# A triangular inverse's transposed products: every second block written to the other half of the partitions

## The chip, the cores and the metric

The kernel runs on one core of a Trainium2 chip. A core has a matrix engine (TensorE, PE in the profile, with its weight loads as PEld), VectorE (DVE), ScalarE (ACT), GpSimd (POOL) and a queue engine (SP) that issues most transfers. TensorE multiplies 128 partitions by up to 128 columns; it can be used as four quarters of 64 by 64, addressed by the half of the partitions from which the operands come (rows) and the half of the partitions to which the product goes (columns). Products land in PSUM, in banks of 512 f32 per partition. The metric is the time of one execution in microseconds, lower is better; several runs give a median.

## What is computed

One decoder layer on 256 tokens of width 1024. Two branches work on the same normalised input: an RWKV-7 time mixing with 8 heads of 64, and a softmax attention with 8 heads of 64 (with 256 tokens its one block is the causal block itself). They are gated, projected and added, and a gated MLP of width 2816 follows. The change lies in the time mixing, whose core is a recurrence over tokens:

```python
def step(state, inp):
    r_t, w_t, k_t, v_t, a_t, b_t = inp
    sa = jnp.einsum('bhvk,bhk->bhv', state, a_t)
    state = (state * w_t[:, :, None, :] + sa[..., None] * b_t[:, :, None, :]
             + v_t[..., None] * k_t[:, :, None, :])
    return state, jnp.einsum('bhvk,bhk->bhv', state, r_t)
```

The kernel doesn't step through tokens. It cuts the 256 tokens into 4 chunks of 64; in a chunk, the terms `sa` depend on one another through a triangular 64x64 matrix, and solving for them takes the inverse of one such matrix for each of 8 heads and 4 chunks: 32 inverses.

## The kernel before, in words

**The inverse.** The tile `X` holds, for each of the 32 matrices, the inverse as far as it is known, on side 0 plain and on side 1 transposed. Its shape is 128 partitions by 2 sides by 16 slots `u` by 64 columns; a matrix sits in one half of the partitions, `bsl(a)` for `a` of 0 or 1, so two matrices share a slot. Slot `u = 8q + i` belongs to group `q` of two, with `i` from 0 to 7. The diagonal blocks of 16 are inverted first, on VectorE, and brought into place by transfers. Then the blocks are joined to 32 and to 64 by products. `below` (line 764) multiplies the matrices in `G` by side 0 of `X`; `masked` (line 772) keeps the part that belongs to the block below the diagonal, in a tile `P`; `plain` (line 781) makes the product for side 0, and `turned_` (line 789) the one for side 1; `added` (line 777) adds a product from PSUM to `X`. The joining to 64 needs only side 1 at the end, so `plain` is called once and `turned_` four times: line 830 for group 0 and line 836 for group 1 (to 32), line 840 for both (to 64). After that, `X` side 1 is used at line 906 in the loop over the 4 chunks.

`below` and `plain` go through `QA`, the four pairs of row half and column half, so successive products fall into four quarters; each of their two PSUM banks takes the products of one row half. `turned_` reads partitions `bsl(a)` and writes `bsl(a)` of one bank, so it uses two quarters: 16 products (8 slots by 2 halves) of f32 64x64 by 64x64.

**PSUM.** Banks come from three tags: `acc` with 3 buffers for the large projections, `ch` with 3 (function `chp`, called through `bank` in this stage), and `at` with 2 (function `atp`), which the attention uses: its `scores` (line 992) take both `at` buffers for each of three parts, which VectorE (line 1002) and, in two parts, ScalarE (line 1005) empty; its transposes (line 1027) and weighted sums (line 1039) take them later.

**The order of the work.** The Python program runs generators as threads: `chain` (the time mixing), `gn` (its group norms), `att` (the attention) and `bulk` (large projections that fill the time). Each `yield cost, lat` tells the planner how much TensorE time the step took and after how long its results are there; the planner (lines 1118 to 1133) always runs the first thread in the list whose due time has passed, so bulk work fills the waiting time. A bulk step here is the eight matmuls of lines 302 and 304 and the four of line 307, with a cost of 0.33 times 4. The framework then sets each engine's order: by default the program's, but an instruction that is not ready by the framework's own timing (an operand, or a free buffer of its tag) is overtaken by later ones that are. Each engine runs its order strictly. VectorE also splits weights for the bulk work (line 269), ScalarE rounds them (line 259), and both serve the attention's softmax (lines 1010 to 1017).

**Behind the stage.** In the loop over chunks, line 910 and line 909 copy the solved terms, lines 916 and 928 make the new state and the output, lines 856 to 866 normalise it (line 864 on GpSimd), and line 873 transposes it on TensorE.

Of the kernel before, what the change touches and what calls it, by code (L numbers as in the profile page):

```python
# [13 lines left out]
OP = mybir.AluOpType  # L14
# [23 lines left out]
def body(tc, x, positions, norm1_g, w_in, rwkv_mu, w_decay_up, decay_bias, w_aaa_up,  # L38
# [3 lines left out]
    act, dve, pool, pe = nc.scalar, nc.vector, nc.gpsimd, nc.tensor  # L42
    ctx = ExitStack()
    with ctx:
# [9 lines left out]
        def b8(name, shape):  # L54
            return sb.tile(shape, F32, name=name, tag="b8", bufs=5)
# [14 lines left out]
        def acc(name="acc"):  # L70
            return ps.tile([128, 512], F32, name=name, tag="acc", bufs=3)

        def chp(name="ch"):
            return ps.tile([128, 512], F32, name=name, tag="ch", bufs=3)
# [410 lines left out]
        with tc.manual_schedule(engines={E.PE, E.Activation, E.DVE, E.Pool}):  # L485
            p = first_steps()
# [24 lines left out]
        p = acc()  # L511
# [12 lines left out]
        def bsl(q):  # L524

            return slice(64 * (1 - q), 64 * (1 - q) + 64)
# [28 lines left out]
        def chain():  # L555
# [35 lines left out]
            p = chp("pss")  # L591
            for t in range(2):
                for ct in range(4):
                    i = 8 * t + 2 * ct
                    pe.matmul(p[:, i:i + 2], sq[:, ct, t * 128:t * 128 + 128], bones[:, 0:128:64],
                              start=True, stop=True)
# [9 lines left out]
            for j in range(2):  # L606
                p = chp("prx").rearrange("p (a t c) -> p a t c", a=2, t=2)
# [59 lines left out]
            for g in range(2):  # L667
                pg = [[p.rearrange("p (u i) -> p u i", u=4) for p in pj] for pj in banks("pgr")]
                for ct in (2 * g, 2 * g + 1):
                    for c in range(4):  # L670
                        u = 4 * ct + c
                        for q, hs in PAR:
                            pe.matmul(pg[ct % 2][q][:, c], kb(q, u), AR[hs, u].rearrange("p a i -> p (a i)"),
                                      start=True, stop=True)
# [39 lines left out]
            X = b8("X", [128, 2, 16, 64])  # L714
# [21 lines left out]
            for c in range(4):  # L736
                for ct in range(4):
                    for q, hs in PAR:
                        pe.matmul(pv[c // 2][hs, c % 2, ct], ch4(zv)[hs, ct, c], ident[hs, hs],
                                  start=True, stop=True)  # L740
# [20 lines left out]
            def bank(nm):  # L761
                return chp(nm).rearrange("p (u n) -> p u n", u=8)

            def below():
                p = [bank("pp") for _ in range(2)]
                for i in range(8):
                    for q, a in QA:
                        u = 8 * a + i
                        pe.matmul(p[q][bsl(a), i], G[q][bsl(q), u, 0:64], X[bsl(q), 0, u], start=True, stop=True)
                return p  # L770

            def masked(p, mk):
                P = b2("P", [128, 8, 64])
                dve.tensor_tensor(P, p, mk[:, None, :].to_broadcast([128, 8, 64]), op=OP.mult)
                return P

            def added(side, g, p):
                v = X[:, side, 8 * g:8 * g + 8]
                dve.tensor_tensor(v, v, p, op=OP.add)

            def plain(P):

                p = [bank("px") for _ in range(2)]
                for i in range(8):
                    for q, a in QA:
                        pe.matmul(p[a][bsl(q), i], X[bsl(a), 1, 8 * q + i], P[q][bsl(a), i], start=True, stop=True)
                return p

            def turned_(q, P):

                p = bank("px")
                for i in range(8):
                    for a in range(2):
                        pe.matmul(p[bsl(a), i], P[bsl(a), i], X[bsl(a), 1, 8 * q + i], start=True, stop=True)
                return p

            yield 0, 11.0
            yield 0, 2.0
# [5 lines left out]
            for j in range(2):  # L804
                p, pg = chp(), chp("pg")
# [21 lines left out]
            P = [masked(pp[q], m16) for q in range(2)]  # L827
            yield 1.4, 2.0
            px = plain(P)
            pt = turned_(0, P[0])  # L830
            for a in range(2):
                added(0, a, px[a])
            added(1, 0, pt)
            yield 2.4, 2.5
            pp = below()
            pt = turned_(1, P[1])
            P = [masked(pp[q], m32) for q in range(2)]
            added(1, 1, pt)
            yield 2.4, 2.5
            pt = [turned_(q, P[q]) for q in range(2)]  # L840
            for q in range(2):
                added(1, q, pt[q])
            yield 2.3, 2.5

            ny = {}
            yah_, yal = by("yah", dt=F32R), by("yal", dt=F32R)
# [38 lines left out]
            for c in range(4):  # L885
# [4 lines left out]
                if St is not None:  # L890
                    for j in range(2):
                        for q, a in QA:
                            ct = 2 * j + a
                            pe.matmul(pz[q][bsl(a), j], AR[half(q), 4 * ct + c, 0], St[half(q), ct],
                                      start=j == 0, stop=False, skip_group_check=True)
                    for j in range(2):
                        for q, a in QA:
                            ct = 2 * j + a
                            pe.matmul(py[q][half(a), j], AR[half(q), 4 * ct + c, 1], St[half(q), ct],
                                      start=False, stop=False, skip_group_check=True)  # L900
# [3 lines left out]
                for j in range(2):  # L904
                    for q, a in QA:
                        pe.matmul(pu[a][bsl(q), j], X[bsl(a), 1, 8 * q + 4 * j + c], Z0[bsl(a), q, c, j],
                                  start=St is None and j == 0, stop=False, skip_group_check=True)
# [4 lines left out]
                if c < 3:  # L912
                    pS = chp("pS").rearrange("p (a n) -> p a n", a=8)
                    for h in range(8):
                        ct, q = divmod(h, 2)
                        pe.matmul(pS[half(q), ct], KBt[c][:, ct, half(q)], VU[:, c, q, ct],
                                  start=True, stop=True)
# [7 lines left out]
                for j in range(2):  # L925
                    for q, a in QA:
                        ct = 2 * j + a
                        pe.matmul(py[q][half(a), j], G[q][:, gslot(ct, c), 64:128], VU[:, c, q, ct],
                                  start=False, stop=j == 1, skip_group_check=True)
# [187 lines left out]

        now_t = 0.0
        threads = [["chain", chain(), 0.0], ["bulk", bulk(), 0.0]]
        while threads:  # L1120
            th = next((h for h in threads if h[2] <= now_t), None)
# [112 lines left out]
        for j in range(11):  # L1234
# [13 lines left out]
            for m in range(2):  # L1248
                n = 2 * j + m
# [29 lines left out]
        for f, is_ in ((0, (0,)), (1, (0,)), (0, (1,)), (2, (0,)), (1, (1,)), (2, (1,)), (3, (0, 1)), (4, (0, 1))):  # L1279
            t, hf = divmod(min(f, 3), 2)  # L1280
            ts = slice(t * 128, t * 128 + 128)
            c0, n = ((0, 512), (0, 256), (256, 256))[max(f - 2, 0)]
# [37 lines left out]
```

## Time and profile before

| what | value |
| --- | --- |
| median of 3 runs (410.5 to 411.31) | 411.17 us |
| profiled execution, its own time | 410.45 us |
| its span, first to last instruction | 408.5 us |
| TensorE busy | 402.3 us, 98% |
| VectorE, ScalarE busy | 325.3 us (80%), 232.3 us (57%) |
| granted TensorE clock, mean | 1.000 |

A row of the timeline gives the start and the duration in microseconds, the engine, the line, the operation, out<-in, the tile of the array (as `64*64`), partitions x elements and, behind `x`, how many records were merged; in brackets stands the idle time of the engine before it and what ended it. A row of the chain gives start, duration, engine, tile and line. A row of the groups has, behind the bar, the busy time in us and the mean of one in ns.

### The profile page before, as it was taken

To read this page: it belongs to the slowest core of one execution; us is meant where nothing else is said; L and a number is where in the kernel's file an instruction comes from. 1 tells how busy PE (TensorE), PEld (TensorE's weight loads), DVE (VectorE), ACT (ScalarE), POOL (GpSimd) and SP (SyncE) were. 2 spreads that over 40 slices of the span, in tenths; PEclk is the share of its full clock that TensorE was granted. 3 is DMA by queue.
4 is the path that set the end of the run, shared out by engine and by line. 5 is a ranking of instruction groups with operands and counts; after the bars stand their busy time and mean duration, and the time that the engine had idled before them with its cause. 6 is when DMAs were issued, how large, how long until landed. Compare 5 with 4: busy or idle time off the path is not lost.

```text
span 408.5 us, 8160 instructions
## 1 busy us (share of the span) xinstructions
PE 402.3 (98%) x3202; PEld 354.8 (87%) x3202; DVE 325.3 (80%) x565; ACT 232.3 (57%) x387; POOL 39.8 (10%) x65
## 2 busy tenths in 40 slices
PE   8999999999999999999999999999999999999996
PEld 4999989888988989999988888888888888888885
DVE  3988999889679786777974899968769678697694
ACT  6799655474546756444553876645545555465450
POOL 8900070000500010020010100000000000000000
PEclk9999999999999999999999999999999999999999
DMA  8944555563783353466663556666665656656612
GB/s 248 311 160 155 156 164 157 149 170 93 167 230 95 102 154 104 131 206 189 197 194 121 174 188 195 217 208 184 209 179 171 215 186 197 203 164 206 200 53 103
DMA packets 61990, 70.53 MB, mean 173 GB/s; under 512 B 9421, under 2 KB 52243, under 8 KB 61952
## 3 DMA queue, kind: packets, MB, share of 16 engines
q1 hardware_dynamic: 61104, 69.54, 56.7%
q0 software_dynamic: 832, 0.47, 0.6%
q8 instruction: 25, 0.41, 0.4%
q14 instruction: 13, 0.11, 0.1%
q10 hardware_dynamic: 16, 0.00, 0.0%
HBM read 68.56 MB, written 1.44 MB: 171 GB/s over the span
## 4 chain that ended last, share of the span: by engine, by line
PE 94%; DVE 2%; ACT 2%; issue 1%; POOL 0%; ACTq 0%
PE acc L1206 15%; PE acc L302 8%; PE acc L1211 8%; PE acc L304 8%; PE acc L307 7%; PE at L1206 5%; PE acc L323 5%; PE acc L327 4%; PE f L1228 4%; PE acc L324 4%; PE f L1230 4%; PE f L1226 4%; PE at L1211 2%; PE acc L461 1%; PE idle L109 1%
## 5 line engine op out<-in xcount | busy, mean ns | idle before, releaser
L259 ACT CAST whi<-raw 128x1024 fp32r<-128x1024 f32 x120 | 125.7, 1051 | 114.1 <-PE acc L1206 22.2
L269 DVE TENSOR_TENSOR wlo<-raw,whi 128x1024 fp32r<-128x1024 f32 x121 | 148.3, 1229 | 30.0 <-PE acc L1211 12.2
L1206 PE MATMUL acc<-hx,whi 128*128 128x512 f32 x264 | 68.2, 393 | 0.0
L302 PE MATMUL acc<-hx,whi 128*128 128x256 f32 x232 | 59.1, 290 | 0.0
L304 PE MATMUL acc<-hx,whi 128*128 128x256 f32 x232 | 56.6, 279 | 0.0
L1206 PEld LDWEIGHTS acc<-hx,whi 128*128 128x128 f32 x264 | 47.0, 188 | 8.1
L302 PEld LDWEIGHTS acc<-hx,whi 128*128 128x128 f32 x232 | 43.7, 188 | 2.1 <-issue 1.2
L304 PEld LDWEIGHTS acc<-hx,whi 128*128 128x128 f32 x232 | 43.7, 188 | 0.1
L1211 PEld LDWEIGHTS acc<-h,wlo 128*128 128x128 f32 x264 | 37.1, 188 | 3.6
L1211 PE MATMUL acc<-h,wlo 128*128 128x256 f32 x264 | 37.9, 279 | 0.0
L307 PE MATMUL acc<-hx,wlo 128*128 128x256 f32 x232 | 36.0, 278 | 0.0
L1228 PE MATMUL f<-whi,hb 128*128 128x512 f32 x80 | 31.2, 390 | 0.0
L1230 PE MATMUL f<-wlo,hb 128*128 128x512 f32 x80 | 31.2, 390 | 0.0
L1226 PE MATMUL f<-whi,hb 128*128 128x512 f32 x80 | 31.2, 389 | 0.0
L307 PEld LDWEIGHTS acc<-hx,wlo 128*128 128x128 f32 x232 | 31.0, 189 | 0.0
L1206 PE MATMUL at<-hx,whi 128*128 128x512 f32 x88 | 24.0, 392 | 0.0
L1216 DVE TENSOR_REDUCE an<-acc 128x256 f32<-128x512 f32 x22 | 14.2, 685 | 9.3 <-PE acc L1211 9.3
L1206 PEld LDWEIGHTS at<-hx,whi 128*128 128x128 f32 x88 | 16.4, 188 | 3.6
L323 PE MATMUL acc<-whi,hx 128*128 128x512 f32 x48 | 19.1, 398 | 0.0
L324 PE MATMUL acc<-whi,hx 128*128 128x512 f32 x48 | 18.7, 390 | 0.0
L1230 PEld LDWEIGHTS f<-wlo,hb 128*128 128x128 f32 x80 | 15.0, 188 | 3.1
L1226 PEld LDWEIGHTS f<-whi,hb 128*128 128x128 f32 x80 | 15.0, 188 | 2.8
(324 smaller groups left out, 698.6 us busy)
## 6 DMA issues: line engine op xcount, KB each, us to landing
raw<-in_w_ffn_up_dram SPq DMA_DIRECT2D x44, 512.0 KB, 4.0
raw<-in_w_in_dram SPq DMA_DIRECT2D x37, 512.0 KB, 4.4
raw<-in_w_ffn_down_dram SPq DMA_DIRECT2D x22, 512.0 KB, 3.9
raw<-in_w_out_dram SPq DMA_DIRECT2D x8, 512.0 KB, 3.8
x<-in_x_dram SPq DMA_DIRECT2D x8, 256.0 KB, 4.2
early<-in_w_in_dram SPq DMA_DIRECT2D x4, 512.0 KB, 7.6
raw<-in_w_branch_b_dram SPq DMA_DIRECT2D x4, 512.0 KB, 3.6
raw<-in_w_branch_a_dram SPq DMA_DIRECT2D x4, 512.0 KB, 4.8
```

The source lines that it names most:

```text
L259: act.copy(wide(hi, k, c), spread(raw, k, c))
L269: eng.tensor_tensor(wide(lo, k, c), spread(raw, k, c), wide(hi, k, c).bitcast(F32), op=OP.subtract)
L302: pe.matmul(om, wh[:, k, ms], xh[:, k0 + k], start=k0 + k + m == 0, stop=False, skip_group_check=True)
L304: pe.matmul(om, wh[:, k, ms], xl[:, k0 + k], start=False, stop=False, skip_group_check=True)
L307: pe.matmul(om, wl[:, k, ms], xh[:, k0 + k], start=False, stop=k0 + k == nk - 1 and m == n - 1, skip_group_check=True)
L323: pe.matmul(ps_[t], xh[:, K, ts], wh[:, k], start=K == 0, stop=False)
L324: pe.matmul(ps_[t], xl[:, K, ts], wh[:, k], start=False, stop=False)
L1206: pe.matmul(ps_[m], wh[:, k, m * 128:m * 128 + 128], hx[:, k0 + k].rearrange("p a s -> p (a s)"), start=k0 + k == 0, stop=False, skip_grou ...
L1211: pe.matmul(ps_[m][:, 0:S], wl[:, k, m * 128:m * 128 + 128], h2[k0 // 4][:, k], start=False, stop=k0 + k == 7, skip_group_check=True)
L1226: pe.matmul(fin[f], hb[:, 0, i, ts], wh[:, 0, cs], start=st, stop=False, skip_group_check=f == 3)
L1228: pe.matmul(fin[f], hb[:, 1, i, ts], wh[:, 0, cs], start=False, stop=False, skip_group_check=f == 3)
L1230: pe.matmul(fin[f], hb[:, 0, i, ts], wl[:, 0, cs], start=False, stop=False, skip_group_check=f == 3)
```

## The change

`turned_` takes two banks instead of one, one of tag `ch` and one of tag `at`, each holding 4 slots. Slots with even `i` go to the first bank, into the same half of the partitions as before; slots with odd `i` go to the second bank, into the other half. A new function `crossed` takes the place of `added` for side 1: one add of 4 slots over all 128 partitions for the even slots, and for the odd ones two adds of 4 slots, each over 64 partitions, which read PSUM in one half and `X` in the other. The three yields behind the products get other costs and due times.

```diff
             def turned_(q, P):
 
-                p = bank("px")
+                p = [f("px").rearrange("p (u n) -> p u n", u=8) for f in (chp, atp)]
                 for i in range(8):
                     for a in range(2):
-                        pe.matmul(p[bsl(a), i], P[bsl(a), i], X[bsl(a), 1, 8 * q + i], start=True, stop=True)
+                        pe.matmul(p[i % 2][bsl(a ^ i % 2), i // 2], P[bsl(a), i], X[bsl(a), 1, 8 * q + i],
+                                  start=True, stop=True)
                 return p
+
+            def crossed(q, p):
+                v = X[:, 1, 8 * q:8 * q + 8:2]
+                dve.tensor_tensor(v, v, p[0][:, 0:4], op=OP.add)
+                for a in range(2):
+                    v = X[bsl(a), 1, 8 * q + 1:8 * q + 8:2]
+                    dve.tensor_tensor(v, v, p[1][bsl(1 - a), 0:4], op=OP.add)
@@
             pt = turned_(0, P[0])
             for a in range(2):
                 added(0, a, px[a])
-            added(1, 0, pt)
-            yield 2.4, 2.5
+            crossed(0, pt)
+            yield 1.9, 2.8
             pp = below()
             pt = turned_(1, P[1])
             P = [masked(pp[q], m32) for q in range(2)]
-            added(1, 1, pt)
-            yield 2.4, 2.5
+            crossed(1, pt)
+            yield 1.9, 2.8
             pt = [turned_(q, P[q]) for q in range(2)]
             for q in range(2):
-                added(1, q, pt[q])
-            yield 2.3, 2.5
+                crossed(q, pt[q])
+            yield 1.2, 2.8
```

## The prediction

> **What bounds the kernel now.** First the page's busy times, then the matmul engine's rows in order of time, then its waits, then the chain of work that ended last.
>
> ```profile
> PE 402.3 (98%) x3202; PEld 354.8 (87%) x3202; DVE 325.3 (80%) x565; ACT 232.3 (57%) x387; POOL 39.8 (10%) x65
> ...
> q8 instruction: 25, 0.41, 0.4%
> ```
>
> PE is the bound: busy in 402.3 of 408.5 us. Work taken off it counts, unless it then waits. The timeline of PE shows the stage of the change (each f32 matmul appears as two records, so the 16 products of one `turned_` call are 32):
>
> ```profile
> 114.29 1.16 PE L769 MATMUL pp<-X,G 64*64 64x64 f32 x64
> ...
> 117.35 1.16 PE L999 MATMUL ps<-qkT,qkT 64*128 64x128 f32 x16
> 118.44 1.16 PE L786 MATMUL px<-P,X 64*64 64x64 f32 x64
> 119.42 0.75 PE L794 MATMUL px<-X,P 64*64 64x64 f32 x20
> 120.56 0.56 PE L794 MATMUL px<-X,P 64*64 64x64 f32 x12 [0.39 <-issue]
> 121.06 0.39 PE L302 MATMUL acc<-hx,whi 128*128 128x256 f32 x1
> ...
> 124.09 1.16 PE L769 MATMUL pp<-X,G 64*64 64x64 f32 x64
> 125.07 0.98 PE L794 MATMUL px<-X,P 64*64 64x64 f32 x28
> 126.21 0.33 PE L794 MATMUL px<-X,P 64*64 64x64 f32 x4 [0.16 <-issue]
> 126.47 1.13 PE L999 MATMUL ps<-qkT,qkT 64*128 64x256 f32 x8
> ...
> 130.47 2.08 PE L794 MATMUL px<-X,P 64*64 64x64 f32 x64
> 132.48 0.38 PE L302 MATMUL acc<-hx,whi 128*128 128x256 f32 x1
> ...
> 148.40 0.41 PE L873 MATMUL pc<-ident,yc 128*128 128x128 f32 x2 [0.75 <-DVE yc L866]
> ```
>
> Line 786 uses four quarters and gets through 64 records from 118.44 to 119.42: 15 ns each. Line 794 uses two and needs 130.47 to 132.48 for 64: 31 ns each. After its start-up PE stands still three times in the whole run, and all three are in these rows: 0.39 and 0.16 us inside line 794, for no wait that the profile names, and 0.75 us at line 873, the group norm's transposes, for VectorE. How that last wait comes about is in the chain that ended last:
>
> ```profile
> 129.90 1.06 ACT whi L259
> 130.95 0.28 ACT sc L1005
> 131.25 1.23 DVE mx L1010
> ...
> 133.19 1.68 ACT sc L1014 x7
> ...
> 137.46 0.34 DVE sc L1002
> ...
> 146.76 1.05 POOL st L864
> 147.83 0.43 DVE yc L866
> ...
> 148.40 0.41 PE pc L873 x2
> 148.81 0.12 PE acc L302
> ```
>
> From about 129 to 148.4 us the chain runs over ACT and DVE (attention's softmax and, behind it in the queues, the first group norm), not over PE. So **the changed products lie just ahead of a stretch in which PE has 0.75 us to spare**; after 148.4 us PE never waits again. The end moves by as much as the row at 148.40 moves, corrected for bulk work done before it.
>
> **The change, part by part.** *The array.* If all four quarters run at line 786's pace, each of the four calls takes 0.5 us for 1.0: 128 records times (31 - 15) ns = -2.0 us of PE. That price is of the same tile size, type and order of quarters as lines 769 and 786, so I take it whole; the lower bound is no saving.
>
> [...] Lines 769 and 786 give each row half its own bank, while the new code lets both row halves write both banks. [...]
>
> ```profile
> 158.33 0.87 PE ppt L1027 x8
> ```
>
> A full-array f32 record of 128 columns takes 0.87 / 8 = 109 ns here, so one of 64 columns would take 54 if it were alone; line 794's 31 are less, so its two quarters already overlap in one bank.
>
> *The first call's gap.* 6404 matmuls and loads over 25 instruction transfers are 256 each, 128 pairs; from the gap before 120.56 to the one before 126.21 lie 12 + 24 + 64 + 28 = 128 records. So both gaps look like the wait for the next block of code. The first is bound to a time (120.5), not to PE: the 20 records ahead of it gain 0.31 us and the gap grows by 0.31. The second gap of 0.16 goes, by the next point.
>
> *The planner.* After the first product step the chain is due again in 2.8 instead of 2.5. A bulk step costs 0.33 x 4 = 1.32, so two of them (2.64) covered 2.5 and do not cover 2.8: a third runs before `below`. Following the due times on, every later step keeps its order. So one bulk step moves ahead of line 873. It is no added work; its length is the distance from 148.81 above to the row below, 1.38 us.
>
> ```profile
> 150.19 0.11 PE acc L302
> ```
>
> *The second bank.* `turned_` now takes one of the two `at` buffers, which the attention scores (line 999) take both of. This is a wait that was not there. VectorE's rows:
>
> ```profile
> 120.14 1.28 DVE L1002 TENSOR_TENSOR sc<-ps,cmask 128x512 f32<-128x512 f32 x2
> ...
> 122.59 1.87 DVE L779 TENSOR_TENSOR X<-X,px 128x512 f32<-128x512 f32 x3
> 124.38 0.16 DVE L1011 TENSOR_SCALAR mx<-mx 128x8 f32<-128x8 f32 x1
> ...
> 125.59 1.28 DVE L774 TENSOR_TENSOR P<-pp,m 128x512 f32<-128x512 f32 x2
> 126.78 0.68 DVE L779 TENSOR_TENSOR X<-X,px 128x512 f32<-128x512 f32 x1
> 127.80 0.20 DVE L1016 RECIPROCAL sm<-sm 128x8 f32<-128x8 f32 x1 [0.34 <-ACT sc L1014]
> 128.03 1.23 DVE L1017 TENSOR_TENSOR sc<-sc,sm 128x1024 f32<-128x1024 f32 x1
> 129.18 0.75 DVE L1002 TENSOR_TENSOR sc<-ps,cmask 128x256 f32<-128x256 f32 x2
> ...
> 134.88 0.18 DVE L1016 RECIPROCAL sm<-sm 128x4 f32<-128x4 f32 x1 [1.02 <-ACT sc L1014]
> ```
>
> The first call's odd products need the first score bank read: 120.14 + 0.68 = 120.8, while PE is there at 119.5. With 28 records left it ends near 121.2, against 121.06 now: the first call gives nothing (+0.5 back, which covers the 0.31 above too). The second call finds its bank free. But the scores behind it need that bank back: masks (1.28 us from 126.6) and then the adds, to about 129.0, while PE is there at 127.1. That is at most 1.9 us. The pair of calls needs the scores read, and the last scores, one bulk step behind the pair, need six adds done: about 1 us. Behind a PE wait stands the whole in-order engine, bulk matmuls first. These waits total 0 to 4 us: 0 if bulk matmuls are placed ahead of the blocked ones, which the trace shows elsewhere: line 1027's second group, which needs an `at` buffer too, stands inside a bulk step (between lines 304 and 302).
>
> ```profile
> 154.68 0.11 PE acc L304
> 154.79 0.64 PE ppt L1027 x4
> 155.43 0.12 PE acc L302
> ```
>
> Split scores then lose their overlap, under 0.5 us each. I take 1.0 beside the first call.
>
> *VectorE.* Each call's add of 0.62 (1.87 / 3) becomes three adds of 256 elements. No row shows one that reads PSUM in the other half; bounds for a half add are a copy of half the partitions and half that width (273 ns), and the full 512-wide add of line 779 (0.68 us above):
>
> ```profile
> L910 DVE COPY VU<-pb 64x128 f32<-64x128 f32 x4 | 0.9, 273 | 0.0
> L693 DVE TENSOR_TENSOR xgh<-xg,xgh 32x256 fp32r<-32x256 f32 x2 | 0.8, 418 | 0.0
> ```
>
> So 0.27 to 0.68 each; the nearest is 0.42 at 32 partitions (fewer partitions do not shorten it), 0.37 back to back as at line 1002. A call costs 1.1 instead of 0.62: +2.0 us of DVE in all (0.9 to 4.4). The page's share would hide it, but here it stands in the chain: +0.5 ahead of line 1011, whose exponentials now end at 128.3; masks and adds, a bulk step later, hold lines 1016 and 1017 until about 129; so the next scores are read 0.5 to 1.2 us later. The pair's +1.0 falls partly into the 1.02 us for which DVE waits before the next line 1016. I take **0.9 us for line 866 and so for line 873**.
>
> [...]
>
> **The sum**, in the profiled execution (span 408.5, time 410.45, 0.72 below the 411.17 median of the runs). PE, which is there at 148.40 - 0.75 = 147.65 now, reaches line 873 at 147.65 + 1.38 - 2.0 + 0.5 - 0.16 + 1.0 = 148.4. Its data come at 148.40 + 0.9 = 149.3: the later one decides. The end moves by 149.3 - 148.40 - 1.38 = **-0.5 us**: 409.95 by its own time, 410.7 by the median. Most of the saving is spent waiting at line 873.
>
> **Rivals.** *All of it arrives*: the instructions' placing puts line 873 or the blocked scores behind more bulk work, so PE never waits: -2.0 and the gaps, some banks lost: -1.2 to -2.2, say -1.8, 409.4. For it: line 1027's case; against it: the present 0.75 us wait was not placed away. *The shared bank makes it slower*: scores in place wait for the adds, 1.9 us and then 1 to 2 us, while PE stands. The place is the two lines 999 behind the calls; it decides once these waits pass 2.4 us, because then PE reaches line 873 (147.4 and the waits) after 148.40 + 1.38 = 149.78. With 4 us, PE is there at 147.4 + 4 = 151.4 and the end is 151.4 - 149.78 = +1.6; with 3.5, +1.1: 412.3. For it: the buffers are two and DVE's queue there is full; against: placement. *No fourfold overlap*: array saving nought, DVE's cost stays: without waits for banks PE arrives at 147.65 + 1.38 - 0.16 = 148.9, with 1.5 us of them at 150.4; the data come at 149.3, so the end moves by -0.5 to +0.6, say +0.3, 411.5. Against it: line 769.
>
> **How the numbers follow.** A measurement here tells about 0.2% (0.8 us) from no change. Most of it lost at line 873: 0.47, own range 409.9 to 411.3, of which 0.10 is faster than that bound. All of it: 0.26, faster. Shared bank: 0.20, of which 0.18 is slower. No overlap: 0.07, of which 0.02 is slower. Sum: faster 0.36, same 0.44, slower 0.20. The range runs from the second case's middle to the third's: 409.1 to 412.3.
>
> **What would show it.** Line 794's records 15 to 16 ns apart right; 31 would mean no overlap. Three bulk steps between the first call and `below`. Adds near 0.4 us. Line 873 waiting 0.9 us or more says that the saving went there; no wait there means the second case; idle time at line 999 or 794 put to DVE means the third. The forecast is wrong if placement shifts other stages, which I cannot read from this trace.

## The result, and the profile after

The change makes the kernel slower: a median of 416.19 us over 4 runs (415.79 to 417.26), against 410.84 (409.96 to 411.31) for the kernel before, also over 4 runs. The ratio is 1.0134, with a 95% interval of 1.0111 to 1.0156. That is 5.4 us slower where 0.5 us faster was forecast, and above the range's 412.3. The profiled execution took 416.06 us (410.45 before). In the experiments below, one run of e2 took 804.8 us, for a reason that the record doesn't show, and isn't counted.

In the rows below, lines behind the changed functions have moved: line 999 is now 1007, 1002 is 1010, 1010 is 1018, 1016 and 1017 are 1024 and 1025, 866 and 873 are 874 and 881. Line 800 is the add of the even slots, line 803 the two half adds of the odd ones.

First the page of the kernel after: the span, the busy times, and the granted clock in 40 slices (the clock that TensorE was given, in tenths of full speed; 9 is 90% or more).

```profile
span 414.3 us, 8169 instructions
...
PE 404.2 (98%) x3202; PEld 356.2 (86%) x3202; DVE 329.1 (79%) x573; ACT 232.6 (56%) x387; POOL 38.8 (9%) x65
...
PEclk9999999999999899999999999999999999999999
```

The span grew by 5.8 us, but TensorE's busy time grew too, by 1.9, although its instructions are the same 3202 and the changed products became shorter. Something makes other matmuls longer, and the one slice with a clock of 8 says where to look. The matmul engine's rows in order of time, through the stage:

```profile
115.14 1.16 PE L769 MATMUL pp<-X,G 64*64 64x64 f32 x64
...
120.27 0.28 PE L794 MATMUL px<-X,P 64*64 64x64 f32 x4
121.39 0.68 PE L794 MATMUL px<-X,P 64*64 64x64 f32 x28 [0.83 <-DVE sc L1010]
...
126.43 1.16 PE L769 MATMUL pp<-X,G 64*64 64x64 f32 x64
127.41 0.65 PE L794 MATMUL px<-X,P 64*64 64x64 f32 x32
127.99 1.13 PE L1007 MATMUL ps<-qkT,qkT 64*128 64x256 f32 x4
129.05 0.38 PE L302 MATMUL acc<-hx,whi 128*128 128x256 f32 x1
...
133.03 1.32 PE L1007 MATMUL ps<-qkT,qkT 64*128 64x256 f32 x4 [2.79 <-DVE X L803]
134.28 1.22 PE L307 MATMUL acc<-hx,wlo 128*128 128x256 f32 x4
...
137.66 1.16 PE L794 MATMUL px<-X,P 64*64 64x64 f32 x64
138.75 0.38 PE L302 MATMUL acc<-hx,whi 128*128 128x256 f32 x1
...
140.33 0.69 PE L1007 MATMUL ps<-qkT,qkT 64*128 64x256 f32 x2
141.65 1.10 PE L1007 MATMUL ps<-qkT,qkT 64*128 64x256 f32 x6 [0.63 <-DVE mx L1019]
...
155.68 0.41 PE L881 MATMUL pc<-ident,yc 128*128 128x128 f32 x2 [0.54 <-DVE yc L874]
```

The array did nearly what was forecast: the pair of calls takes 137.66 to 138.75, 1.09 us for 64 records, where it took 2.01; the second single call takes 0.58 for 32. But TensorE stops 0.83, 2.79 and 0.63 us, and each time it is held by the second bank: the first call waits until VectorE has read the scores, then twice the scores wait for VectorE. And four bulk matmuls of line 307 need 1.22 us at 134.28, where a whole bulk step of twelve took 1.38 before. The windows (stretch, its length, busy time and count of PE, its loads, VectorE, ScalarE, GpSimd; then the granted clock as a share of full speed, the DMA share and GB/s) show why:

```profile
133.00:134.00 1.00, 0.96 (x4) 0.67 (x4) 0.34 (x1) 0.37 (x1) 0.00 (x0) 0.89 0.00 0
134.00:135.00 1.00, 1.00 (x4) 0.72 (x4) 0.42 (x1) 0.15 (x1) 0.00 (x0) 0.50 0.00 0
...
133.90:137.30 3.40, 3.40 (x16) 3.02 (x15) 1.64 (x2) 0.38 (x2) 0.00 (x0) 0.52 0.00 0
...
138.00:139.00 1.00, 1.00 (x59) 0.93 (x51) 1.00 (x2) 0.34 (x1) 0.00 (x0) 1.00 0.00 0
```

Right behind the stop of 2.79 us the array runs at half its clock for some 3.4 us, which loses about 1.7 us of work. TensorE counts as busy in all of the 3.40 us, at a clock of 0.52, so the page's 98% hides this.

Why the stop is so long stands in VectorE's rows:

```profile
125.58 2.35 DVE L269 TENSOR_TENSOR wlo<-raw,whi 128x1024 fp32r<-128x1024 f32 x2
128.93 0.20 DVE L1024 RECIPROCAL sm<-sm 128x8 f32<-128x8 f32 x1 [1.00 <-ACT sc L1022]
129.17 1.23 DVE L1025 TENSOR_TENSOR sc<-sc,sm 128x1024 f32<-128x1024 f32 x1
130.41 1.29 DVE L774 TENSOR_TENSOR P<-pp,m 128x512 f32<-128x512 f32 x2
131.61 0.41 DVE L800 TENSOR_TENSOR X<-X,px 128x256 f32<-128x256 f32 x1
132.04 0.85 DVE L803 TENSOR_TENSOR X<-X,px 64x256 f32<-64x256 f32 x2
132.92 0.42 DVE L1010 TENSOR_TENSOR sc<-ps,cmask 128x256 f32<-128x256 f32 x1
```

`below` is done at 127.4, but its masks (line 774) start at 130.41. In VectorE's order of instructions the softmax's reciprocal and division now stand **ahead** of the masks; before, the masks came first (125.59) and the division after them (128.03). VectorE waits 1.00 us for ScalarE's exponentials, divides, and only then masks and adds; the scores get their bank at 132.9. TensorE, also in order, has bulk work only until about 130.2.

**The balance**, between line 769 and line 881, which lay 34.11 us apart and now lie 40.54 apart. The bulk step that moved into it accounts for 1.38, which comes back behind line 881; +5.05 stay. Waits: 0.83 + 2.79 + 0.63 + 0.54 = 4.79 for 0.39 + 0.16 + 0.75 = 1.30, +3.49. Half clock: +1.7. Array: -1.9 (without their stops the first call, the second and the pair took 1.25, 1.24 and 2.01, and take 0.90, 0.58 and 1.09). The remaining 1.8 fits the scores: eight records at line 999 in one go took 1.13; cut in two by the bank they take 1.13 + 1.32, and for the last part 0.69 + 1.10, together +2.0, of which 0.2 is the half clock once more. The other 0.8 of the span is the later start, 115.14 for 114.29, before any changed instruction; the wait at line 414, far ahead of the stage, alone runs from none (before) to 1.6 us (e7 below), so I don't count it to the change.

### The profile page after: what moved, and what is told of

Read it like the earlier page. It is cut to its first block, busy times and chain, and to the rows that moved or that the text cites. A ratio compares the mean times of both kernels' runs of the same rounds, so it can differ in the third digit from the quotient of the medians.

```text
span 414.3 us, 8169 instructions
## 1 busy us (share of the span) xinstructions
PE 404.2 (98%) x3202; PEld 356.2 (86%) x3202; DVE 329.1 (79%) x573; ACT 232.6 (56%) x387; POOL 38.8 (9%) x65
## 4 chain that ended last, share of the span: by engine, by line
PE 83%; DVE 7%; DMA 5%; SPq 2%; issue 1%; ACT 0%; POOL 0%; DVEq 0%; ACTq 0%
PE acc L1214 15%; PE acc L302 8%; PE acc L1219 7%; PE acc L307 7%; PE acc L304 7%; PE at L1214 5%; PE f L1236 4%; PE f L1238 4%; PE f L1234 4%; PE acc L323 3%; PE acc L324 3%; PE acc L327 3%; DVE wlo L269 3%; PE at L1219 2%; DMA raw<-in_w_in_dram 2%; SPq L720 2%
## 5 line engine op out<-in xcount | busy, mean ns | idle before, releaser
L302 PE MATMUL acc<-hx,whi 128*128 128x256 f32 x232 | 59.7, 292 | 0.0
L304 PE MATMUL acc<-hx,whi 128*128 128x256 f32 x232 | 57.3, 281 | 0.0
L307 PE MATMUL acc<-hx,wlo 128*128 128x256 f32 x232 | 37.0, 282 | 0.0
```

Source lines behind the costliest of these rows:

```text
L302: pe.matmul(om, wh[:, k, ms], xh[:, k0 + k], start=k0 + k + m == 0, stop=False, skip_group_check=True)
L304: pe.matmul(om, wh[:, k, ms], xl[:, k0 + k], start=False, stop=False, skip_group_check=True)
L307: pe.matmul(om, wl[:, k, ms], xh[:, k0 + k], start=False, stop=k0 + k == nk - 1 and m == n - 1, skip_group_check=True)
```

## The experiments

The theory after this profile: three things have to come together. The faster array brings TensorE early to a bank it shares with the attention; the extra bulk step, which the new due times call for, shifts the division ahead of the masks; the cut adds load VectorE. Rivals: the shared bank alone, the due times alone, the added VectorE work alone, or the clock. All twelve kernels compute the whole layer. "Before" is the median of the kernel before in the same job. The ratio and its interval are estimated from all the counted runs, and can differ by 0.1% from the quotient of the two medians; differences in us in the text are the ratio's, times 411.

| run | median us | before us | ratio (95%) |
| --- | --- | --- | --- |
| e1_acc | 413.81 | 410.96 | 1.0079 (1.006 to 1.0098) |
| e2_yields | 410.86 | 410.96 | 1.0003 (0.9992 to 1.0014) |
| e3_bank | 411.63 | 410.96 | 1.0021 (1.0008 to 1.0033) |
| e4_oldyields | 411.74 | 410.96 | 1.0019 (1.0009 to 1.003) |
| e5_adds_yields | 412.14 | 410.56 | 1.0029 (1.0014 to 1.0044) |
| e6_acc_oldyields | 410.60 | 410.56 | 0.9996 (0.9983 to 1.0009) |
| e7_fill | 414.98 | 410.56 | 1.0116 (1.0089 to 1.0144) |
| e8_pair | 410.68 | 410.56 | 1.0003 (0.9991 to 1.0015) |
| e9_order | 412.05 | 410.52 | 1.0043 (1.0028 to 1.0059) |
| e10_order_acc | 412.74 | 410.52 | 1.0063 (1.0037 to 1.009) |
| e11_pool_before | 411.12 | 410.52 | 1.0013 (0.9996 to 1.003) |
| e12_pool_acc | 410.99 | 410.52 | 1.0015 (1.0003 to 1.0026) |

### The second bank from another tag

The kernel after, with the second bank of `turned_` from the projections' tag:

```diff
-                p = [f("px").rearrange("p (u n) -> p u n", u=8) for f in (chp, atp)]
+                p = [f("px").rearrange("p (u n) -> p u n", u=8) for f in (chp, acc)]
```

> The changed kernel with one word changed: the second bank of the turned products comes from the acc buffers (3, for the large projections) and not from the at buffers that the attention scores use. Theory 1 (the scores behind the second turned product wait on PE for its bank, 2.8 us, and the array's clock falls behind that wait): no idle row at line 1007, granted clock 1.00 all through, 4.5 to 6.5 us of the 5.4 come back, -1.5 to +0.8 us against the kernel before. Theory 2 (VectorE's eight extra adds are what costs): still +3 us or more, as the adds are all there. Theory 3 (the new due times, by one more bulk step ahead of below): still +3 us or more.

It gives back 2.3 us (1.0134 to 1.0079, times 411), and no score waits for a bank any more. But 3.2 us remain, where theory 1 expected 0.8 at most. TensorE stops further on, at the new state of the recurrence, for the late copies of the solved terms (here lines 917 and 918). The matmul engine's rows and the windows:

```profile
142.43 0.33 PE L924 MATMUL pS<-VU,KBt 128*64 128x64 f32 x2 [1.33 <-ACT VU L917]
143.61 1.01 PE L924 MATMUL pS<-VU,KBt 128*64 128x64 f32 x13 [0.86 <-DVE VU L918]
```

```profile
143.00:150.00 7.00, 6.39 (x51) 6.27 (x52) 4.63 (x11) 3.33 (x11) 0.00 (x0) 0.51 0.55 153
150.00:152.00 2.00, 2.00 (x44) 1.81 (x44) 1.37 (x2) 1.83 (x3) 0.00 (x0) 1.00 0.00 0
```

Again the clock halves, now for nearly 7 us, which loses about 3.4 in this execution (415.05 us, the longest of the six; its mean clock is 0.991, as in one other, while the remaining four have 0.996). So the bank shared with the scores isn't the whole cause, and the half clock isn't tied to that place.

### The due times alone

The kernel before, with nothing but the new yields (`yield 1.9, 2.8` twice, `yield 1.2, 2.8`):

> The kernel before with only the three new yields: two quarters, one bank, four plain adds. Theory 1: no shared bank, so within 0.8 us of before; the group norm's wait on PE may move by some tenths. Theory 2: within 0.8 us. Theory 3 (due times alone): +3 us or more.

No difference: 1.0003. The extra bulk step by itself costs nothing, since on TensorE it only changes places. But it already turns VectorE's order round: the division stands ahead of the masks.

```profile
128.02 1.22 DVE L1017 TENSOR_TENSOR sc<-sc,sm 128x1024 f32<-128x1024 f32 x1
129.16 1.28 DVE L774 TENSOR_TENSOR P<-pp,m 128x512 f32<-128x512 f32 x2
```

Here no score stands for it, since none needs a bank from the calls. The same order stands in e1, e5 and e7, which have the new due times too; in e3, e4, e6 and e8, where the step ahead of `below` keeps its old due time, the masks come first, as before.

### The bank alone

The kernel before, in its two quarters and with its due times, but every odd slot in a bank of tag `at`, and each add cut into two:

```diff
-                        pe.matmul(p[bsl(a), i], P[bsl(a), i], X[bsl(a), 1, 8 * q + i], start=True, stop=True)
+                        pe.matmul(p[i % 2][bsl(a), i // 2], P[bsl(a), i], X[bsl(a), 1, 8 * q + i],
+                                  start=True, stop=True)
```

> The kernel before with only the second bank: odd slots go to an at buffer, in the same half of the partitions, so two quarters as before, and two adds of four slots each in place of one of eight; old yields. Theory 1: PE waits at the scores for the bank, but less than 2.8 us, since without the extra bulk step VectorE's order has the masks ahead of the softmax division: +0.5 to +2.5 us. Theory 2: four more adds of about 0.1 us each beyond what they replace: within 0.8 us. Theory 3: within 0.8 us.

Slower by 0.9 us (1.0021). There is no stop at the scores; they are split (four records from 126.95, four from 128.56), and there is no wait at the group norm's transposes; the transposes come 34.97 us after line 769 where they came 34.11 after it. So the bank has a price, but a sixth of what the change costs.

### All of the change, with the due times of before

```diff
             crossed(0, pt)
-            yield 1.9, 2.8
+            yield 2.4, 2.5
...
             crossed(1, pt)
-            yield 1.9, 2.8
+            yield 2.4, 2.5
...
-            yield 1.2, 2.8
+            yield 2.3, 2.5
```

> The changed kernel with the yields of before: four quarters, the at bank and the crossed adds all in, only the extra bulk step out. Theory 1 as refined (the wait is long because the extra bulk step puts masks and adds behind the softmax division in VectorE's order): the wait at line 1007 falls from 2.8 to about 1 us, the clock stays at 1.00, and the time is -0.7 to +1.5 us against before. Theory 2: still +4 us or more. Theory 3: about -1 us, with the wait gone.

1.0019: 4.7 of the 5.5 us (1.15% of 411) come back, though the array, the bank and the cut adds are all in it. The masks stand ahead of the reciprocal again:

```profile
125.40 1.29 DVE L774 TENSOR_TENSOR P<-pp,m 128x512 f32<-128x512 f32 x2 [0.30 <-PE pp L769]
...
127.81 0.19 DVE L1024 RECIPROCAL sm<-sm 128x8 f32<-128x8 f32 x1
```

The stops at the scores are 0.26 and 0.31 us, and no clock is lost in the stage. The three due times cost nothing alone and 4.7 us here, so neither they nor the bank can be priced by themselves.

### The cut adds and the due times, without the fourfold array

Two quarters and one bank as before; each add cut into three of the new sizes, without crossing halves; the new yields:

```diff
+            def thirds(g, p):
+                v = X[:, 1, 8 * g:8 * g + 8:2]
+                dve.tensor_tensor(v, v, p[:, 0:8:2], op=OP.add)
+                for a in range(2):
+                    v = X[bsl(a), 1, 8 * g + 1:8 * g + 8:2]
+                    dve.tensor_tensor(v, v, p[bsl(a), 1:8:2], op=OP.add)
```

> The kernel before (two quarters, one ch bank) with the new yields and with each add of eight slots cut into three as in the changed kernel, but without crossing halves. Theory A (what costs is that TensorE, 2 us faster, meets VectorE and ScalarE work that is later, stops for over 2 us and loses its clock): TensorE is not faster here, so it waits 1 to 2 us in short pieces, the clock stays at 1.00, +0.3 to +1.5 us. Theory B (late adds and due times suffice, whatever the array does): a stop of 2 us and the clock at half behind it as with the acc bank, +2.5 to +4 us.

1.0029, +1.2 us. Its waits (engine, tile and line, what it waited for: us in total, times, longest):

```profile
PE pc L880 <- DVE yc L873: 1.1, 1, 1.1
...
PE pS L923 <- DVE VU L917: 0.8, 1, 0.8
```

The added VectorE work reaches TensorE as later data for the group norm, as the prediction had it, and for the recurrence, which it didn't name. It isn't enough for 5.4 us.

### Four quarters without the shared bank and with the old due times

Both edits of e1 and e4 together:

> Four quarters and crossed adds, the second bank from acc, the yields of before: neither shared bank nor extra bulk step. Theory A: waits on TensorE of 1.5 us at most in all, clock 1.00, -0.8 to +0.5 us against before. Theory B (the adds alone make VectorE late): +2 us or more.

0.9996: level, though TensorE waits longer than the 1.5 us that were expected. This is the array's saving with the least of the change's costs around it, and nothing arrives:

```profile
PE px L794 <- issue: 1.7, 1, 1.7
...
PE pc L881 <- DVE yc L874: 0.5, 1, 0.5
PE pS L924 <- DVE VU L918: 0.4, 1, 0.4
PE px L794 <- ACT gt L1081: 0.3, 1, 0.3
```

2.9 us of waits for 1.3: in this execution 1.6 of the 1.9 by which the products became shorter are spent standing. Most of it is 1.7 us in the first call, for no wait that the profile names, where 0.39 stood before; the rest is late VectorE data, and 0.3 for the new bank, which ScalarE still reads for the projections (`gt`, line 1081). The first call's stop can't be put down to the change, though: it is 1.38 us in e8, whose first call is that of before, and 0.26 in e12, whose first call is this one. So what takes the saving in the median run isn't shown.

### Filling the stop

The kernel after, with twelve 512-column matmuls on a tile of ones ahead of the second part's scores. They add work, into a bank that nobody reads; the question was whether the clock stays when TensorE has something to do.

```diff
             for i, part in enumerate(parts):
+                if i == 1:
+                    fill = acc("fill")
+                    for _ in range(12):
+                        pe.matmul(fill, ones[:, 0:128], ones, start=True, stop=True)
                 scores(*part)
```

> The changed kernel with twelve bf16 matmuls of 512 columns by the ones tile (0.22 us each, as long as the 2.8 us for which TensorE stands at line 1007) ahead of the second part's scores, into an acc bank that nobody reads. If the half clock comes from the standing still, it stays at 1.00 there and about 2 us of the 5.4 come back: +2 to +4 us against before; a wait may open behind it, as the placement changes. If the half clock has another cause (the four quarters, say), the fillers only add work: +5 to +8 us.

Inconclusive. The matmul engine's rows, then the windows:

```profile
128.93 2.54 PE L1059 MATMUL fill<-ones 128*128 128x512 bf16 x11 [0.16 <-issue]
...
133.64 1.10 PE L1007 MATMUL ps<-qkT,qkT 64*128 64x256 f32 x6 [1.54 <-DVE X L803]
```

```profile
134.00:135.00 1.00, 1.00 (x8) 0.64 (x5) 0.62 (x2) 0.16 (x1) 0.00 (x0) 0.91 0.00 0
135.00:138.00 3.00, 3.00 (x16) 3.00 (x16) 1.59 (x3) 1.43 (x5) 0.00 (x0) 0.50 0.00 0
```

A stop of 1.54 us was left, and the clock halved all the same, for as long. But this execution (417.76 us, mean clock 0.994) is the longest of six. One more has 0.994 (416.61 us); the other four have 0.998 to 1.000 and took 414.31 to 415.00, so they lost little or nothing to the clock and were still some 4 us slower than before. In the kernel after, all four runs have 0.992 to 0.996. This points to the standing still as what lowers the clock, but in so few runs it isn't shown. The ratio, 1.0116, can't be told from that of the change.

### VectorE's order put back

The kernel after, all of it, with one addition: the reciprocal and the division of the first softmax part may be issued only behind the second call's adds.

```diff
+                with ExitStack() as held:
+                    if t == 0:
+                        held.enter_context(tc.issue_after(last_cross[3]))
+                    dve.reciprocal(sm, sm)
+                    dve.tensor_tensor(sc, sc, sm[:, :, None].to_broadcast([128, nh, nk]), op=OP.mult)
```

> The changed kernel, all of it (four quarters, at bank, crossed adds, new yields), with one order forced: the first softmax part's reciprocal and division on VectorE stand behind the second call's masks and crossed adds, not ahead of them. Theory C (the extra bulk step let the division overtake masks and adds, and TensorE stood for them): the masks start when the product below is done, the wait at line 1008 (the second scores) falls from 2.8 us to under 0.8, the clock stays at 1.00, and 3.5 to 5 us of the 5.4 come back: +0.3 to +1.8 us against before, near the kernel with the old yields. Theory D (the shared bank with more adds is enough, in whatever order): still +3.5 us or more.

1.0043: 3.7 us (0.91% of 411, give or take 1.1 by the two intervals) come back, and nothing about the array, the bank, the adds or the due times was touched. VectorE's rows, the matmul engine's and two windows (lines are one further on):

```profile
128.58 1.29 DVE L775 TENSOR_TENSOR P<-pp,m 128x512 f32<-128x512 f32 x2
...
130.98 0.19 DVE L1029 RECIPROCAL sm<-sm 128x8 f32<-128x8 f32 x1
```

```profile
122.00 0.68 PE L795 MATMUL px<-X,P 64*64 64x64 f32 x28 [1.69 <-DVE sc L1011]
...
131.21 1.10 PE L1008 MATMUL ps<-qkT,qkT 64*128 64x256 f32 x4 [0.74 <-DVE sm L1029]
```

```profile
130.00:134.00 4.00, 3.26 (x24) 2.70 (x23) 3.50 (x8) 1.67 (x3) 0.00 (x0) 1.00 0.57 189
134.00:140.00 6.00, 5.35 (x93) 4.26 (x92) 5.11 (x11) 2.46 (x7) 0.00 (x0) 1.00 0.34 90
```

The masks start at 128.58, not 130.41; the stop at the scores is 0.74, not 2.79; and the clock stays at 1.00. **This is the cause of the larger part of the loss**: an instruction of another thread, waiting for ScalarE, stood ahead of the masks in a queue that is served in order. With the long stop the half clock behind it is gone too, in all seven runs (0.999 or 1.000). What is left, 1.8 us, fits the bank's other stops (here 1.69 and 0.65) and the split scores, less the array's saving.

### The order and the other bank together

Both edits, e9's and e1's:

> The same forced order with the second bank from acc: four quarters, crossed adds, new yields, no shared bank. Theory C: the clock stays at 1.00 and the 3.3 us of the acc version with new yields go: -0.8 to +0.8 us against before. Theory D: still +2.5 us or more.

1.0063, slower by 2.6 us, outside what was expected. The matmul engine's rows and one window:

```profile
141.65 0.33 PE L925 MATMUL pS<-VU,KBt 128*64 128x64 f32 x2 [1.08 <-ACT VU L918]
142.68 0.70 PE L925 MATMUL pS<-VU,KBt 128*64 128x64 f32 x13 [0.71 <-DVE VU L919]
```

```profile
143.00:147.00 4.00, 4.00 (x42) 3.88 (x41) 3.97 (x6) 3.33 (x11) 0.00 (x0) 0.57 0.43 114
```

With the scores out of the way TensorE runs into the late copies, as in e1, and in this execution the half clock costs 1.7 us again. That doesn't explain the 2.6 us: four of the eight runs have a mean clock of 0.994 to 0.996 and took 412.18 to 416.31 us, the other four 0.998 to 1.000 and 411.66 to 413.82, hardly faster by their medians (412.74 and 412.50). What makes this kernel slower than expected stays open; its interval overlaps that of e9.

### Four quarters in the last pair of calls only

The first two calls as before; the pair writes both groups into two banks of tag `ch`, so that an add spans 512 elements again, and no bank is shared with the attention:

```diff
+            pt = [bank("px") for _ in range(2)]
+            for i in range(16):
+                for a in range(2):
+                    pe.matmul(pt[i % 2][bsl(a ^ i % 2), i // 2], P[i // 8][bsl(a), i % 8], X[bsl(a), 1, i],
+                              start=True, stop=True)
+            v = X[:, 1, 0:16:2]
+            dve.tensor_tensor(v, v, pt[0], op=OP.add)
+            for a in range(2):
+                v = X[bsl(a), 1, 1:16:2]
+                dve.tensor_tensor(v, v, pt[1][bsl(1 - a)], op=OP.add)
```

> A version meant to be better: two quarters and one bank in the first two calls as before, with their yields; only the last two calls use four quarters, the even slots of both groups in one ch bank and the odd ones in another (two ch banks, as before), with one add of 512 and two half adds of 512 for both groups; its yield is 1.3, 2.8. Array -1.0 us, VectorE +0.6 us. Theory A: no new wait over 1 us, clock 1.00, -1.0 to +0.2 us. Theory B: VectorE's half adds alone make it slower, +0.5 us or more.

1.0003: level. It has half of the saving and few of the costs, and TensorE waits at the same later places (0.59 us for the copies, 0.64 at the group norm), besides 1.38 us in the first call, which is that of before.

### The divisions on GpSimd

If VectorE's queue is the place, taking the divisions of two softmax parts off it should let TensorE's saving through. In the kernel before (e11) and in e6 (e12):

```diff
-                dve.tensor_tensor(sc, sc, sm[:, :, None].to_broadcast([128, nh, nk]), op=OP.mult)
+                eng = pool if (t, j) != (1, 1) else dve
+                eng.tensor_tensor(sc, sc, sm[:, :, None].to_broadcast([128, nh, nk]), op=OP.mult)
```

> The kernel before with the softmax divisions of the first two parts (128x1024, 1.22 us of VectorE each, not needed for over 10 us) on GpSimd. A control: VectorE's queue is what holds the group norm's wait of 0.75 us, so about 0.5 us of it goes: -0.8 to +0.3 us. If GpSimd's work holds up VectorE's, +0.5 us or more.

> Four quarters, crossed adds, acc bank, old yields, and the two divisions on GpSimd. If the 2.0 us that the array saves are lost to waits for VectorE (as theory A says of the version with the acc bank and old yields, which came out level), taking 2.4 us of work off VectorE ahead of those waits sets 0.8 to 2 us free: -2.0 to -0.8 us against before. If the waits have other causes (code transfers, ScalarE), no better than -0.5.

1.0013, which can't be told from no difference, and 1.0015: e12 gains nothing of the 0.8 to 2.0 us that it should have by its first theory. The group norm's wait is gone in both, but others stand in its place. The waits of e11, then of e12:

```profile
PE pb L906 <- DVE Z L902: 1.2, 1, 1.2
```

```profile
PE px L794 <- ACT gt L1082: 1.3, 1, 1.3
PE pb L914 <- DVE Z L910: 1.2, 1, 1.2
```

In e12 the 1.3 us are a wait for the bank again: ScalarE reads the projection in it (`gt`), and the products go on near 132.5. In this stretch several chains of small steps end at nearly the same time. Taking one out shows the next.

## Why the prediction was wrong, by its own steps

**The array**: right. The forecast was 31 to 15 ns a record and -2.0 us; the pair of calls needs 1.09 us for 64 records, 17 ns each, the second single call 18, with modelled ends counted in, and the four calls together save 1.9. The rival without fourfold overlap falls: both row halves write both banks here, and still all four quarters overlap, at 17 ns a record where two quarters took 31.

**The planner**: right in what it counted. Three bulk steps run between the first call and `below`, and they are no added work (e2: 1.0003). What it left out is that the step changes the order on another engine: `below` comes later against the softmax, and the framework puts the division ahead of the masks, in e2 already.

**The second bank**: this is the step that failed, "I take 1.0 beside the first call". The three stops are 0.83, 2.79 and 0.63 us. The first was forecast: the first call waits for the scores to be read and ends at 122.0, where 121.2 was forecast for a stage that began 0.85 us earlier. The third was put at about 1 us. The second was bounded by "masks (1.28 us from 126.6) and then the adds, to about 129.0", at most 1.9 us; the masks came at 130.41 and the adds ended at 132.89, some 3 us later than that even with the later start taken off. The bound assumed the order of before on VectorE, in which the masks precede line 1016. The hope set against it, "0 if bulk matmuls are placed ahead", came true in part only: bulk matmuls stand between 129.05 and 130.2, then TensorE has nothing left that its order lets through. The splitting of the scores was priced too low as well: "under 0.5 us each", measured 1.3 (0.2 of it half clock) and 0.7.

**The rival with the shared bank** named the mechanism and the place: waits past 2.4 us at the scores behind the calls. They were 3.42 us, 4.25 with the first call's. What it said of line 873, that TensorE would then come there later than its data, didn't happen: TensorE still waits 0.54 us there. Its price, +1.1 to +1.6, was too small for two reasons: it granted no loss by the clock (1.7 us) and little by split scores (1.8).

**VectorE**: nearly right in the adds. They take 0.41 and 0.42 each, 1.28 a call against a forecast of 1.1; by themselves, with the due times, they make the kernel 1.2 us slower (e5), through the group norm's wait, which was named, and the recurrence's, which wasn't.

**"Most of the saving is spent waiting at line 873"**: that the saving doesn't arrive holds in e6 and e8, which are level, without the `at` bank and with the old due time ahead of `below`. But line 873 isn't the place: its wait is 0.5 and 0.6 us there, below the 0.75 of before, and 0.54 in the kernel after. That the saving arrives whole is refuted for these versions.

**The clock** was in no step: the sum puts it at nothing without a reason, and it cost 1.7 us. Its mean of 1.000 stood in the table before; that a stop could cost more than its length was not asked.

**The range**: its lower end is called the second case's middle, which the prediction itself puts at 409.4, and it says 409.1. Nothing hangs on this here.

What stays open: what exactly lowers the clock (below), what takes the saving in e6, and why e10 is slower than expected. No run has the `at` bank, the new due times and the cut adds with only two quarters, so it isn't shown that the faster array is needed for the loss. That the order decides most of it is shown by e9 and e4, and that the new due times turn the order by e2; the reason, that the extra step makes `below` later than the division, is worked out from the rows, not from the framework's own times.

## What to carry to other kernels

Here an engine that is 98% busy gained nothing from 1.9 us of shorter work while its neighbours' data came no earlier: before pricing a saving, read which later instruction waits and what its producer does meanwhile. When a change takes a buffer that another thread uses, work out the order of **every** in-order queue anew for the new arrangement, above all what waits for a third engine ahead of the instruction that frees the buffer, and don't bound the wait by the old order. A due time that crosses a multiple of the filling step isn't a detail: it cost nothing alone and 4.7 us in company.

## What the runs showed of the hardware

**Half the clock around short stops, in four profiled executions.** The largest idle time of TensorE within any 3.4 us of the profiled executions (the length of three of the four low spells), summed from the windows in steps of 0.2 us from 110 to 155 us: 2.79 in the kernel after, 2.19 in e1, 1.78 in e10 and 1.54 in e7. In all four the granted clock fell to 0.50: 0.8 us behind the end of the stop in the kernel after, 0.6 in e10, 1.2 in e7, and in e1 within the second of its two stops. In e9 (1.70), e6 (1.65), e8 (1.37) and the kernel before (0.75) it stayed at 1.00, and so it did in the other six, with 1.33 at most (e12). The first four lie from 130 us on, those of e9, e6 and e8 near 120. One bound for all doesn't fit, since 1.54 fell and 1.70 didn't; what else counts wasn't settled. The low spells lasted 3.4 us, and 6.8 in e1. Nor does every run of a kernel do the same: by their mean clocks only two of six runs of e7 and four of eight of e10 were lowered. (These means are rough: one run of e3 has 0.949 at 412.59 us, a time that shows no such loss.)

**The two half adds didn't overlap.** Two adds of 64 partitions by 256, which start in other halves, take 0.85 us (line 803, 0.42 each), where two of 128 by 256 with the same start took 0.75 (line 1002 in the prediction, 0.41 to 0.42 each). So a half add is no cheaper than a whole one of that width, 0.42 against 0.41 (line 800). The pair thus ends 0.10 us later than that one.

**Four quarters share two banks at nearly the pace of line 786**: 64 records in 1.09 us, with products of both row halves in each bank, where line 786, with a bank for each row half, takes 0.98.
